# Three of four MLP halves with seven block products instead of eight, and the partial sums copied between PSUM banks

## The chip, the cores and the metric

The kernel runs on all 8 cores of one Trainium2 chip, every core with its own 2048 prompt tokens and 16 sample tokens and the same weights. The metric is the device time of the slowest core, in microseconds. Most executions of a kernel agree within a few tenths of a per cent. In some, the cores of one die, or of both, run at a lower granted TensorE clock and the time is some per cent to 18% longer; such runs are called slow and are left out.

## The reference, cut to what matters

```python
D_MODEL, SEQ, DEPTH = 1024, 2048, 2        # D_FF = 4 * D_MODEL
for l in range(DEPTH):
    h = rmsnorm(x, norm_mix[l])
    mixed = even_layer(h, ...) if l % 2 == 0 else odd_layer(h, ...)   # pool + recurrence / short convolution
    x = x + mixed
    h = rmsnorm(x, norm_mlp[l])
    x = x + jnp.square(jax.nn.relu(h @ ff_w1[l])) @ ff_w2[l]          # the part that changes
return rmsnorm(x, norm_final), ...
```

The first output is the prompt's result after the final norm; the others are the sample group's result and the states.

## The kernel before

The program writes its own instruction order: small Python generators yield operations, each with an estimated duration, and a list scheduler picks which one goes next on its engine. `MMG` is a group of matmuls into one PSUM bank, `ACT` an operation of ScalarE, `TT` a two-tensor operation of VectorE.

```python
# the MLP before: up projection, per 512 hidden columns (s) and 512 tokens (t)
for n in range(4):
    k = (yield Alloc(SB))[0]
    yield MMG([(bank(k), ring[:, sl, kc * 512 + n * 128:kc * 512 + (n + 1) * 128],
                hT[:, kc, tokslice(t)], kc == 0, kc == 7) for kc in range(8)], [B_ring[sl], hTb(t)], [B_ps[k]])
    def ev(...):
        yield ACT(hb[n], bank(k), AF.Relu, [B_ps[k]], [Bh[n]])
        banks.give(k)
        yield TT(hb[n], hb[n], hb[n], ALU.mult, [Bh[n]], [Bh[n]], fast=True)      # the square
# down projection: per block of 128 tokens 2 x 4 matmuls of 128x512, added to x_sb by VectorE
# ...
def main():
    yield from outproj(0, U_WO, 1, "mix", range(8), True)
    mlp(0, U_FF0, 1, 2, (0, 1), (0, 1), hid_a, True)          # layer 0, first 1024 tokens
    # ...
    yield from outproj(1, U_WO, 1, "mix", range(8, 17), False)
    mlp(1, U_FF0, 1, 2, (2, 3, 4), (4, 2, 3), hid_b, False)   # layer 0, second 1024 tokens and the sample tokens
    # ...
    yield from conv()
    yield from outproj(1, U_OO, 3, "cmix", range(17), False)
    mlp(1, U_FF1, 3, 4, (0, 1, 2, 3, 4), (4, 0, 1, 2, 3), hid_b, False)   # layer 1, all tokens
```

## Time and profile before

| | before |
|---|---|
| median of 13 runs | 1563.57 us (fast runs 1560.92 to 1565.59) |
| TensorE busy | 96% of the span, 1495.8 us |
| VectorE, ScalarE busy | 59%, 38% |
| weights read by the GpSimd queue | 74.00 MB, 27.1% of the queue's 16 engines |

The span can be cut into five stages at matmuls that are easy to find: the first and longest (recurrence, first half of layer 0), then the second half of layer 0's MLP ("X"), the convolution and its output projection, layer 1's MLP ("Y") and the tail. The windows of the kernel before, slowest core; the columns are length, then busy time and number of PE, PEld, DVE, ACT and POOL, then clock, DMA share and GB/s:

```profile
0.00:603.20 603.20, 553.34 (x3878) 299.41 (x3878) 426.92 (x781) 334.11 (x716) 159.38 (x176) 0.98 0.51 107
603.20:849.70 246.50, 243.75 (x1689) 121.34 (x1688) 117.99 (x158) 57.34 (x110) 17.99 (x34) 0.99 0.39 69
849.70:1090.80 241.10, 236.66 (x1378) 114.33 (x1376) 139.95 (x236) 91.61 (x169) 9.53 (x18) 1.00 0.21 38
1090.80:1554.20 463.40, 461.96 (x2684) 219.75 (x2680) 234.42 (x297) 102.48 (x202) 13.76 (x26) 1.00 0.21 44
1554.20:1563.60 9.40, 0.11 (x1) 0.00 (x0) 5.16 (x5) 3.11 (x8) 0.00 (x0) 0.68 0.55 224
```

In X and Y, which the change concerns, TensorE is busy for all but 2.8 and 1.4 us. These two stages are 710 of 1564 us.

### The profile page before, as it was taken

What the parts mean: (1) busy time and instruction counts of PE and PEld (TensorE: products, weight loads), DVE (VectorE), ACT (ScalarE), POOL (GpSimd) and SP (SyncE); (2) the same over time, 40 slices, a digit from 0 to 9 for tenths busy, and PEclk for the clock granted to TensorE, in tenths of its full rate; (3) what the DMA queues carried; (4) which work ended last, traced back from release to release, by engine and by line L of the source; (5) the groups of instructions that cost most, each with busy time, mean ns of one, the idle gap of its engine ahead of it and who ended that gap; (6) DMA issues with size and microseconds to landing.
All of it is one profiled execution on the core that took longest, in us unless ns stands there. A gap on an engine that the chain in (4) does not pass through costs nothing.

```text
span 1563.6 us, 24713 instructions; the slowest of 8 cores (1553.1 to 1563.6 us)
## 1 busy us (share of the span) xinstructions
PE 1495.8 (96%) x9620; PEld 754.8 (48%) x9620; DVE 924.4 (59%) x1475; ACT 588.7 (38%) x1201; POOL 200.7 (13%) x254
## 2 busy tenths in 40 slices
PE   3888899999999999999998999999999999999997
PEld 2555455654444445444454444445444444444453
DVE  4799788877545565444446655556444444444457
ACT  4767588864211174111116222256211111111135
POOL 1143533333200000000000000000000000000000
PEclk9899899999999999999999999999999999999999
DMA  6843144388743532443442012330231132031013
GB/s 157 179 85 64 61 89 95 76 200 181 162 86 56 91 70 55 73 84 62 74 69 41 15 27 50 54 69 1 54 54 28 27 54 40 16 55 28 1 56 162
DMA packets 57070, 113.39 MB, mean 73 GB/s; under 512 B 5822, under 2 KB 32556, under 8 KB 56940
## 3 DMA queue, kind: packets, MB, share of 16 engines
q0 software_dynamic: 21344, 74.00, 27.1%
q1 hardware_dynamic: 33996, 37.48, 7.9%
q8 instruction: 79, 1.29, 0.4%
q10 hardware_dynamic: 1616, 0.33, 0.1%
q14 instruction: 35, 0.29, 0.1%
HBM read 170.31 MB, written 15.54 MB: 119 GB/s over the span
## 4 chain that ended last, share of the span: by engine, by line
PE 85%; DVE 7%; DMA 4%; ACT 2%; issue 1%; ACTq 1%; SPq 0%; POOL 0%; DVEq 0%; POOLq 0%
PE pp L523 83%; DMA ring<-wst 2%; PE pp L533 2%; DVE x_sb L492 1%; DVE x_sb L504 1%; DMA mixT<-xs 1%; DVE hT L492 1%; DVE arena L492 1%; ACT arena L479 1%; ACTq L538 1%; ACT x_sb L479 1%; DVE arena L504 1%; DVE x_sb L848 0%; DVE gsm L492 0%; DMA arena<-st_pool 0%
## 5 line engine op out<-in xcount | busy, mean ns | idle before, releaser
L523 PE MATMUL pp<-hT,ring 128*128 128x512 f16 (+1 forms) x4304 | 800.4, 340 | 5.5 <-DMA ring<-wst 3.5
L523 PEld LDWEIGHTS pp<-hT,ring 128*128 128x128 f16 x4304 | 357.9, 98 | 401.5 <-issue 17.8
L492 DVE TENSOR_TENSOR x_sb<-x_sb,pp 128x1024 f32<-128x1024 f32 (+1 forms) x384 | 377.6, 986 | 163.4 <-PE pp L523 159.7
L479 ACT ACTIVATE arena<-pp 128x512 f16<-128x512 f32 (+5 forms) x320 | 181.8, 573 | 619.5 <-PE pp L523 593.4
L523 PE MATMUL pp<-ring,arena 128*128 128x512 f16 x1536 | 340.7, 380 | 3.6 <-DVE arena L492 3.6
L523 PEld LDWEIGHTS pp<-ring,arena 128*128 128x128 f16 x1536 | 150.1, 98 | 185.8 <-issue 6.1
L492 DVE TENSOR_TENSOR arena<-arena 128x512 f16<-128x512 f16 (+1 forms) x206 | 90.8, 441 | 244.0 <-ACT arena L479 243.9
L523 PE MATMUL pp<-ring,mixT 128*128 128x512 f16 x1024 | 231.5, 379 | 3.2 <-DVE x_sb L492 2.6
L538 POOL DMA_DIRECT2D ring<-wst x145 | 78.2, 544 | 1043.3 <-PE pp L523 952.6
L523 PEld LDWEIGHTS pp<-ring,mixT 128*128 128x128 f16 x1024 | 97.6, 98 | 115.3 <-issue 5.4
L480 ACT ACTIVATE arena<-x_sb 128x1024 f16<-128x1024 f32 x64 | 67.5, 1054 | 62.5 <-DVE x_sb L492 46.7
L479 ACT ACTIVATE mixT<-pp 128x512 f16<-128x512 f32 x64 | 38.1, 595 | 131.8 <-PE pp L523 131.7
L492 POOL TENSOR_TENSOR x_sb<-x_sb 128x512 f32<-128x512 f32 (+6 forms) x60 | 73.9, 1231 | 82.2 <-ACT x_sb L479 17.6
L492 DVE TENSOR_TENSOR hT<-pp,gcols_s 128x1024 f16<-128x1024 f16 x64 | 76.9, 1218 | 11.1 <-PE pp L533 11.1
L492 DVE TENSOR_TENSOR mixT<-mixT 128x512 f16<-128x512 f16 x64 | 31.4, 492 | 74.8 <-ACT mixT L479 74.8
L492 DVE TENSOR_TENSOR arena<-pp,arena 128x512 f32<-128x512 f32 (+1 forms) x57 | 39.0, 687 | 42.9 <-PE pp L523 35.6
L479 ACT ACTIVATE x_sb<-x_sb 128x512 f32<-128x512 f32 (+3 forms) x98 | 54.1, 558 | 24.5 <-DVE x_sb L492 15.7
L504 DVE SCALAR_TENSOR_TENSOR arena<-arena,convwf_s 128x512 f32<-128x512 f32 x64 | 47.8, 751 | 20.7 <-ACT arena L479 19.4
L479 ACT ACTIVATE arena<-arena 128x512 f32<-128x512 f32 x88 | 54.3, 622 | 4.9 <-DVE arena L504 3.8
L479 ACT ACTIVATE arena<-x_sb,nrm 128x1024 f16<-128x1024 f32 x48 | 54.4, 1142 | 0.8
L523 PE MATMUL pp<-ring,hT 128*128 128x128 f16 (+1 forms) x832 | 53.4, 223 | 0.5 <-DVE hT L492 0.5
L523 PEld LDWEIGHTS pp<-ring,hT 128*128 128x128 f16 (+1 forms) x832 | 49.3, 99 | 4.0 <-issue 2.1
(134 smaller groups left out, 800.9 us busy)
## 6 DMA issues: line engine op xcount, KB each, us to landing
ring<-wst POOLq DMA_DIRECT2D x137, 512.0 KB, 7.3
x_sb<-xp SPq DMA_DIRECT2D x28, 512.0 KB, 8.6
yp<-x_sb SPq DMA_DIRECT2D x16, 512.0 KB, 2.6
x_sb<-st_hgrn SPq DMA_DIRECT2D x24, 256.0 KB, 3.1
nhs<-x_sb SPq DMA_DIRECT2D x24, 256.0 KB, 2.6
ring<-wst POOLq DMA_DIRECT2D x8, 256.0 KB, 7.2
arena<-gfin SPq DMA_DIRECT2D x1, 512.0 KB, 4.0
nhp<-arena SPq DMA_DIRECT2D x4, 64.0 KB, 1.5
```

What stands on the lines that cost most here:

```text
L479: return e.activation(out=out, in_=in_, func=func, bias=bias, scale=scale)
L480: return e.activation(out=out, in_=in_, func=func, bias=bias, scale=scale, accum_out=accum)
L492: return Op(eng, lambda e: e.tensor_tensor(out=out, in0=in0, in1=in1, op=op), R, W, occ, occ + 0.08)
L504: return Op("dve", lambda e: e.scalar_tensor_tensor(out=out, in0=in0, scalar=scalar, in1=in1, op0=op0, op1=op1), R, W, occ, occ + 0.08)
L523: ins = e.matmul(o, l, r, start=s, stop=t)
L533: ins = e.transpose(out=o, in_=i, identity=idn)
L538: fns = [(lambda e, o=o, i=i: e.dma_start(out=o, in_=i)) for (o, i) in pairs]
```

## The change

The intent is fewer matmuls. A product of two matrices cut into 2 x 2 blocks takes eight block products; Strassen's method in Winograd's form takes seven, and pays with sums of blocks. Here one level of it is used for X and Y. A "quad" of four 128x512 outputs takes 7 x 4 = 28 matmuls instead of 32. Sums of weight blocks and of activation blocks are made on VectorE ahead of the matmuls. The sums behind them are mostly made in PSUM: a product that two outputs share stays in its bank, ScalarE copies it to a second bank, and the next product accumulates onto the copy. One product per quad goes to SBUF and is added by VectorE, with a custom instruction that also clamps.

```diff
+        def quad(prods, evac, pre=None, nxt=None):
+            def bits(k):                      # sets the written bits of a bank that gets a copy
+                if not B_ps[k].full:
+                    yield MMG([(bank(k), identh[:, :], identh[:, :].unsqueeze(1).broadcast_to([128, 4, 128]), True, True)],
+                              [B_const], [B_ps[k]])
+            def copy(k, src):
+                yield from bits(k)
+                yield ACT(bank(k), bank(src), AF.Copy, [B_ps[src]], [B_ps[k]])
+            # ... products 1, 5 | copy | 6 | copy | 2, 7 | next quad's 1 | copy | 3 | 4
+        def wmlp(tag, l, seq, n_in, n_out, smp, gates):
+            # comb1: weight blocks, four sums of 512 a quad      comb2: w2 blocks, four sums of 2048 a group
+            # combh: activations, four sums of 2048 a half       combs: hidden columns, eight sums of 1024 a group
+                        if what in ("12", "22"):
+                            yield Op("dve", lambda e: e._custom_dve(TENSOR_ADD_SAT, out=v, in0=bank(k), in1=gst(n), s0=3e38, s1=0.0), ...)
+        def later_norms(n, blocks, gate_):    # norms of the other half's blocks, made during the last group of a half
+        def warm(on, off):                    # while on, matmuls into a spare bank fill the holes of the planned order
 # ...
-            mlp(0, U_FF0, 1, 2, (0, 1), (0, 1), hid_a, True)
+            mlp(0, U_FF0, 1, (0, 1), hid_a)
-            mlp(1, U_FF0, 1, 2, (2, 3, 4), (4, 2, 3), hid_b, False)
+            wmlp("X", 0, [1], 1, 2, 1, dict(w1c=(), t=(m0,), ...))
+            S.spawn(later_norms(2, range(0, 8), up(("X", "ff2", 2))), FINPRIO)
-            mlp(1, U_FF1, 3, 4, (0, 1, 2, 3, 4), (4, 0, 1, 2, 3), hid_b, False)
+            wmlp("Y", 1, [0, 1], 3, 4, 0, dict(w1c=op3[0:8], t=op3[0:8], ...))
+            S.spawn(later_norms(3, range(8, 16), up(("Y", "ff2", 2))), FINPRIO)
+        S.spawn(warm(up(("op1", 14)), up(("X", "u", 0))), 0)
+        S.spawn(warm(up(("X", "u", 15)), up(("h2", 7), ("X", "done"))), 0)
+        S.spawn(warm(up(("op3", 15)), up(("Y", "u", 0))), 0)
```

Around it, weights come in blocks of 512 KB (layer 1's twice, once per half), banks are no longer reserved in pairs, results are added 512 wide, and the convolution's weights are loaded in another order. This surrounding is called the frame below.

## The prediction

> **What bounds the kernel now.** I first read the busy table of the page and the chain that ended last, then the stages as windows, then single groups of instructions.
>
> ```profile
> PE 1495.8 (96%) x9620; PEld 754.8 (48%) x9620; DVE 924.4 (59%) x1475; ACT 588.7 (38%) x1201; POOL 200.7 (13%) x254
> PEclk9899899999999999999999999999999999999999
> PE 85%; DVE 7%; DMA 4%; ACT 2%; issue 1%; ACTq 1%; SPq 0%; POOL 0%; DVEq 0%; POOLq 0%
> ```
>
> TensorE (PE) is busy 96% of the span at nearly full granted clock, and 85% of the chain is PE. A busy PE need not be at its peak, so I asked for the chain in order of time and for two stages, the second pass of the layer-0 MLP (611 to 833 us) and the layer-1 MLP (1097 to 1544 us).
>
> ```profile
> 611.45 221.77 PE pp L523 x1488
> 840.72 0.68 DVE arena L492 x2
> 841.39 0.14 issue
> 841.53 8.98 PE pp L523 x56
> 1096.94 404.83 PE pp L523 x2344
> ```
>
> ```profile
> 1097.00:1544.00 447.00, 447.00 (x2545) 211.78 (x2545) 221.63 (x283) 92.77 (x179) 12.43 (x24) 1.00 0.20 42
> 611.50:833.00 221.50, 221.50 (x1488) 108.20 (x1487) 103.61 (x140) 42.66 (x80) 14.81 (x28) 1.00 0.39 70
> ```
>
> The window columns are length, then busy time and count of PE, PEld, DVE, ACT, POOL, then clock, DMA share, GB/s. In both MLP stages PE never stops; VectorE (DVE) is half idle, ScalarE (ACT) 80% idle, DMA at 0.2 to 0.4. One matmul is dated from the timeline:
>
> ```profile
> 1210.53 7.07 PE L523 MATMUL pp<-hT,ring 128*128 128x512 f16 x32
> 1212.51 0.60 ACT L479 ACTIVATE arena<-pp 128x512 f16<-128x512 f32 x1 [8.84 <-PE pp L523]
> 1213.14 0.43 DVE L492 TENSOR_TENSOR arena<-arena 128x512 f16<-128x512 f16 x1 [1.80 <-ACT arena L479]
> 1217.43 7.07 PE L523 MATMUL pp<-ring,arena 128*128 128x512 f16 x32
> ```
>
> 32 matmuls start 6.90 us before the next 32, so one costs 0.2158 us. This stage can be shortened only by fewer matmuls, and that is what the change does.
>
> **What the Trainium skill says.** "TensorE: Matmul & The Clock Gate", Part 1, gives 215.7 ns start to start for 512 columns on a warm clock; the 0.2158 us agree. "VectorE: DVE Perf Modes", section on the perf-mode tier table, puts tensor_tensor at 2x for 16-bit operands in SBUF (1224 ns for 2048 elements) and at 1x with a PSUM operand. The trace agrees:
>
> ```profile
> L492 DVE TENSOR_TENSOR x_sb<-x_sb,pp 128x512 f32<-128x512 f32 x168 | 113.8, 684 | 21.0 <-PE pp L523 17.3 <-PE pp L533 1.0
> L492 DVE TENSOR_TENSOR arena<-arena 128x512 f16<-128x512 f16 x192 | 81.5, 425 | 243.9 <-ACT arena L479 243.9
> L479 ACT ACTIVATE arena<-pp 128x512 f16<-128x512 f32 x192 | 114.5, 597 | 515.1 <-PE pp L523 515.0
> ring<-wst POOLq DMA_DIRECT2D x137, 512.0 KB, 7.3
> ```
>
> "PSUM — Partial Sum Buffer", section on the four PSUM rules, says that ACT and DVE writes leave the written bits alone and that a matmul without the start flag adds where the bit is set. The change rests on this (it copies a partial sum to another bank and accumulates onto it). No trace of before shows it; I take the result as correct. "SBUF — State Buffer", section "Who interferes with whom", says tensor_tensor takes only the read half of the port pair that it shares with GpSimd, so the added combinations should not stop the POOL-issued weight loads (inferred there; not shown here).
>
> **The change part by part.** It is Strassen's method in Winograd's form, one level deep: 7 products instead of 8, for the layer-0 MLP on the second 1024 tokens ("X") and the whole layer-1 MLP ("Y"), three of the four MLP halves. The first half of layer 0, which runs beside the recurrence, stays.
>
> Removed: a half has 512 matmuls for each of the two projections. The new unit, a quad, does with 7 x 4 = 28 matmuls what took 32. There are 32 quads in a half, 96 in all, so 96 x 4 = 384 matmuls x 0.2158 = 82.9 us go from PE, all on the path. The small sample-token matmuls keep their number (16 x 16 and 4 x 64 per layer).
>
> Added on ACT: three PSUM-to-PSUM copies in every quad, at an estimated 0.60 us each (the eviction's duration). In the up projection a quad also has one copy of a partial sum and two relus, 6 x 0.60 = 3.6 us of the 28 x 0.2158 = 6.04 us that PE takes, before its share of four squares (0.43 us on DVE, about 0.6 on ACT); with three of four on ACT 5.4 us, 89%. In the down projection it is 1.8 us, 30%.
>
> Added on DVE, per group of 1024 hidden columns (8 quads, 48.3 us of PE): 16 weight combinations of 512 (0.425), 4 of 2048 and 8 of 1024. From the 425 and 684 ns I take a fixed 0.16 us and 0.27 us per 512 at 2x, so about 1.22 and 0.69 us: 6.8 + 4.9 + 5.5. Then 8 custom add-and-clamp reads of PSUM at 0.69 (5.5), 24 residual adds of 0.684 (16.4), four or five squares (1.9), 1.2 for the activation combination. Sum 42.2 of 48.3 us, 87%; the trace shows back-to-back DVE starts 0.06 to 0.08 us closer than the durations, so some 80%. Before it was 50%. Neither engine exceeds PE, but both come close in the up projection.
>
> Added DMA: Y reads its weights twice. A group loads 8 x 512 KB; the POOL queue took 27.1% of 1563.6 us for 74 MB, 5.7 us per MB, so 24 of 48 us. Bandwidth suffices; but four loads issued at once (about 13 us) stand in front of a w1 load that has some 16 us, so it is near.
>
> Latency on the path. A copy's loop is PE to ACT 0.25 us (8 x 0.2158 after 1210.53 is 1212.26; ACT starts at 1212.51), 0.60, and 0.14 back (the issue piece of the chain): 0.99 us. Inside a run of quads two products (1.73 us) cover it: nothing, unless another ACT operation is in front. A run's first quad covers it with one product (0.86): 0.13 to 0.6. Two such starts a group, 24 x 0.3 = 7 us. From up to down projection the last relu, square and four combinations take about 0.25 + 0.6 + 0.43 + 2.8 + 0.14 = 4.2 us, and the next group's first quad (6.0) plus one product covers it: I take 1 us per group for queueing, 12 us.
>
> Ends of stages. X needs all eight norms and four combinations of 2048 (4.9 us) before the second product that runs; before, the stage started after four norms, and the last transposed norm of this outproj came at 612.7, 9.5 us after the last matmul of its outproj: +10 us. X to conv, with eight late norms pushed into the last group: +4. Between Y's halves the combination cannot be done early and nothing covers the hand-over: +5. End of X and of Y without a next quad as cover: +2 each. The tail gets shorter: before, four 1024-wide adds and four final scalings queue on DVE after the last matmuls (1547.2 to 1559.9); after, two blocks per 6 us: -5. Dummy matmuls put into X's start and end and Y's start keep the clock up; they fill idle time only.
>
> Sum: -82.9 + 7 + 12 + 10 + 4 + 5 + 4 - 5 = -45.9, that is 1518 us.
>
> **The rivals.** (1) PE stays the bound throughout, the author's order hides nearly everything: -82.9 + 10 (X's start) + 5 is 1497. For it: 20% slack on DVE, and instruction order fixed from durations close to the trace's. Against: three latency-bound copies per quad behind an 89% busy ACT. (2) ACT and DVE become the bound of the up projection: 3 us more per group as the copies queue, 36 us over my sum, 1554. For it: 89 and 87%. Against: the down projection has slack and the 8 banks allow work ahead. (3) A weight load arrives late in each group, 2 us each: 1542. For it: 13 of 16 us; against: DMA share under half. (4) A granted clock that falls, as stalls let the array idle: 5% of 580 us is 29 us, 1547; against it, stalls of 1 us are short and the page shows 9s in slices with 5 us of idleness.
>
> **Range and chances.** The gain is one number with little doubt, the losses are a sum of small waits between 15 and 85 us. Predicted 1518, range 1490 to 1550. The 2% line is 1533.2; my sum is 15 us below, and the dummy matmuls show waits that somebody measured and tended. Faster by over 2%: 0.73; within 2%: 0.24; slower: 0.03.
>
> **What would show it.** PE at 128x512 with 5632 real matmuls plus dummies instead of 6016; about 201 us for X and 395 to 410 for Y; DVE near 80% and ACT near 70% in both; ACT copies of 0.6 us PSUM to PSUM 288 times; in the waits, PE waiting for ACT's copies (about 7 us) and for the combinations at group changes. It is wrong if the PE idle time inside X and Y exceeds 60 us, if copies take over 0.8 us, if the f16 combinations run at 1x, or if weight loads show as PE's releaser.

## The result and the profile after

The changed kernel is correct and takes 1529.11 us (median of 8 runs, 1524.09 to 1530.06), against 1563.57 of before. The ratio of the two is 0.9774, with a 95% interval of 0.9763 to 0.9784: faster by 2.3%. (A ratio is the mean time of one kernel's fast runs over the mean of the other's fast runs of the same rounds, so it is not quite the ratio of the medians.) The change is 34.5 us, where 45.9 had been predicted; 1529 lies inside the range.

The busy table and the chain that ended last, of the page after:

```profile
PE 1441.5 (95%) x9312; PEld 722.0 (47%) x9334; DVE 1089.1 (72%) x1964; ACT 768.9 (51%) x1558; POOL 223.0 (15%) x286
PE 77%; DVE 7%; DMA 7%; ACT 5%; issue 2%; POOL 1%; SPq 0%; DVEq 0%; ACTq 0%; POOLq 0%
```

TensorE lost 54 us of busy time, not 83, in part because 98 matmuls of 512 columns are not products (below). The same five stages, kernel after, slowest core:

```profile
0.00:601.90 601.90, 548.45 (x3808) 297.56 (x3831) 423.50 (x791) 318.25 (x676) 160.62 (x177) 0.98 0.53 108
601.90:841.30 239.40, 236.67 (x1695) 116.84 (x1693) 180.50 (x320) 136.21 (x271) 16.89 (x31) 1.00 0.39 63
841.30:1073.40 232.10, 232.03 (x1312) 110.79 (x1311) 143.47 (x260) 70.70 (x128) 12.52 (x22) 1.00 0.30 49
1073.40:1511.00 437.60, 423.64 (x2502) 196.72 (x2501) 336.73 (x592) 241.06 (x475) 32.98 (x57) 1.00 0.47 84
1511.00:1522.40 11.40, 0.74 (x4) 0.13 (x2) 4.88 (x7) 2.66 (x8) 0.00 (x0) 0.69 0.44 176
```

X and the convolution stage together lost 16.1 us, Y 25.8; the tail gained 2.0. In Y TensorE now stands still for 14 us; VectorE is busy 77% of it and ScalarE 55%. The groups of instructions that the change added, kernel after, from 560 us on (mean ns of one behind the busy time):

```profile
L493 ACT ACTIVATE pp<-pp 128x512 f32<-128x512 f32 x288 | 166.8, 582 | 209.3 <-PE pp L539 165.2 <-PE pp L541 39.6 <-DVE x_sb L506 2.5
L1697 DVE CUSTOM_DVE_ANT_0 arena<-pp,ring 128x512 f16<-128x512 f32 x84 | 56.2, 686 | 11.6 <-ACT pp L493 7.1 <-PE pp L539 4.3
L506 DVE TENSOR_TENSOR arena<-arena 128x1024 f16<-128x1024 f16 x54 | 37.1, 687 | 2.8 <-ACT arena L493 2.5
L506 DVE TENSOR_TENSOR mixT<-hT,mixT 128x2048 f16<-128x2048 f16 x15 | 18.3, 1220 | 0.0
L1968 PE MATMUL pp<-identh 128*128 128x512 f16 x65 | 16.1, 379 | 0.0
L541 PE MATMUL pp<-identh 128*128 128x512 f16 x33 | 12.5, 384 | 0.0
```

The sizes were as assumed: copies 0.58 us (0.60 assumed), the custom instruction 0.69, the sums 0.69 and 1.22. The last two rows are the matmuls that are no products: 65 that fill holes, and 33 that set the written bits of a bank ahead of a copy. At 0.2158 us start to start the latter are 7.1 us of TensorE, which the prediction had not counted.

TensorE waits, from X to the end, kernel after (engine, line waited for, us in total, times, longest):

```profile
PE pp L539 <- ACT pp L493: 6.8, 12, 1.6
```

So the copies stop TensorE 12 times in 96 quads. The timeline puts nearly all these waits into the groups at the beginnings and ends of a half; between 1339 and 1482 us there is none. A group is 1024 hidden columns; from the start of one down projection to the next it has 224 matmuls, 48.3 us. Three successive such periods of Y, kernel after: the change of halves and the two groups behind it.

```profile
1273.15:1339.24 66.09, 60.36 (x353) 28.52 (x352) 58.52 (x96) 43.54 (x96) 6.51 (x11) 0.97 0.72 145
1339.24:1387.99 48.75, 48.75 (x223) 21.20 (x222) 38.15 (x68) 24.85 (x46) 5.15 (x8) 1.00 0.61 98
1387.99:1436.14 48.15, 48.15 (x223) 21.53 (x222) 38.61 (x69) 25.43 (x46) 3.71 (x7) 1.00 0.40 71
```

The steady groups run at the matmuls' own pace; seven products are worth their full eighth there. The change of halves takes 66 us, with VectorE busy for 58.5 of it: besides the group's own work it makes eight final scalings (10.2 us), four of the late norms' evictions (4.9) and the four sums of activations (4.9). TensorE stands still for 5.7 us, and one of these waits does more than wait:

```profile
1275.73 0.61 PE L551 MATMUL pp<-identh,arena 128*128 128x128 f16 x8 [1.98 <-ACT arena L493]
1276.17 1.75 PE L541 MATMUL pp<-mixT,arena 128*128 128x512 f16 x4
1277.71 1.91 PE L539 MATMUL pp<-mixT,arena 128*128 128x512 f16 x4
```

The eight transposes of a late norm waited 1.98 us for ScalarE's scaling; four matmuls then take 1.75 and 1.91 us instead of 1.02, as the granted clock was halved for 3.4 us from 1276.3 on (the trace's clock record). And the tail on VectorE, kernel after:

```profile
1510.93 2.47 DVE L506 TENSOR_TENSOR x_sb<-x_sb,pp 128x512 f32<-128x512 f32 x4
1515.51 2.48 DVE L518 SCALAR_TENSOR_TENSOR x_sb<-x_sb,nrm,hg 128x1024 f32<-128x1024 f32 x2 [2.10 <-ACT nrm L493]
```

Two blocks finish at the same moment, and their adds, squares and scalings go through one after the other.

### The profile page after: what moved, and what is told of

Same layout as the page of the kernel before. It is cut to its first block, busy times and chain, and to the rows that moved or that the text cites. A ratio compares the mean times of both kernels' runs of the same rounds, so it can differ in the third digit from the quotient of the medians.

```text
span 1522.4 us, 25344 instructions; the slowest of 8 cores (1512.4 to 1522.4 us)
## 1 busy us (share of the span) xinstructions
PE 1441.5 (95%) x9312; PEld 722.0 (47%) x9334; DVE 1089.1 (72%) x1964; ACT 768.9 (51%) x1558; POOL 223.0 (15%) x286
## 4 chain that ended last, share of the span: by engine, by line
PE 77%; DVE 7%; DMA 7%; ACT 5%; issue 2%; POOL 1%; SPq 0%; DVEq 0%; ACTq 0%; POOLq 0%
PE pp L541 51%; PE pp L539 24%; DMA ring<-wst 3%; ACT arena L493 2%; PE pp L551 2%; DVE x_sb L506 2%; ACT arena L494 1%; DMA mixT<-xs 1%; DMA x_sb<-xp 1%; DVE x_sb L518 1%; DVE arena L506 1%; DMA hT<-w2w 1%; ACT x_sb L493 1%; ACT pp L493 1%; DVE mixT L506 1%
## 5 line engine op out<-in xcount | busy, mean ns | idle before, releaser
L541 PE MATMUL pp<-hT,ring 128*128 128x512 f16 (+1 forms) x2704 | 506.6, 336 | 5.7 <-DMA ring<-wst 3.4
L506 DVE TENSOR_TENSOR x_sb<-x_sb,pp 128x512 f32<-128x512 f32 x504 | 335.5, 684 | 127.7 <-PE pp L541 89.9
L541 PEld LDWEIGHTS pp<-hT,ring 128*128 128x128 f16 x2704 | 224.1, 98 | 250.7 <-issue 17.2
L541 PE MATMUL pp<-ring,mixT 128*128 128x512 f16 x1264 | 293.5, 379 | 3.4 <-DVE x_sb L518 1.8
L493 ACT ACTIVATE pp<-pp 128x512 f32<-128x512 f32 x288 | 166.8, 582 | 209.3 <-PE pp L539 165.2
L493 ACT ACTIVATE arena<-pp 128x512 f32<-128x512 f32 (+5 forms) x212 | 117.5, 559 | 159.6 <-PE pp L541 82.1
L539 PE MATMUL pp<-hT,ring 128*128 128x512 f16 x480 | 118.4, 379 | 2.0 <-ACT pp L493 1.0
L493 ACT ACTIVATE arena<-arena 128x512 f32<-128x512 f32 (+1 forms) x176 | 108.8, 625 | 17.6 <-DVE arena L1697 13.0
L506 DVE TENSOR_TENSOR arena<-arena 128x512 f16<-128x512 f16 (+3 forms) x148 | 79.3, 541 | 34.8 <-ACT arena L493 34.3
L539 PE MATMUL pp<-mixT,arena 128*128 128x512 f16 x384 | 95.2, 381 | 0.6 <-ACT pp L493 0.5
L506 DVE TENSOR_TENSOR mixT<-mixT 128x512 f16<-128x512 f16 (+1 forms) x81 | 39.1, 484 | 71.2 <-ACT mixT L493 71.2
L539 PEld LDWEIGHTS pp<-hT,ring 128*128 128x128 f16 x480 | 45.2, 97 | 62.5 <-issue 11.7
```

The lines of the kernel that those rows point to most:

```text
L493: return e.activation(out=out, in_=in_, func=func, bias=bias, scale=scale)
L506: return Op(eng, lambda e: e.tensor_tensor(out=out, in0=in0, in1=in1, op=op), R, W, occ, occ + 0.08)
L539: ins = e.matmul(o, l, r, start=s, stop=t, skip_group_check=True)
L541: ins = e.matmul(o, l, r, start=s, stop=t)
```

## The experiments

Twelve kernels ran, on three chips. "The control" is the changed kernel. Where a kernel has the control's instructions in the control's order, periods between the same two ScalarE instructions can be compared core by core; they are given below for undisturbed cores, worked out from the start times in the traces, and tell more than the whole time, which is a maximum over eight cores.

**The same frame with eight products.** X and Y are computed with plain sums of two products per output; no sums of blocks, no copies, no bit-setting.

```diff
-                    prods = [pr(r.v[:, 0, :], r.B, b11), pr(r.v[:, 1, :], r.B, b21), pr(c.v[:, 2, :], c.rows[2], b22), ...]   # 7
-                    pre = yield from quad(prods, evac, pre, ...)
+                    pairs = [("11", [pr(w11, r.B, b11), pr(w12, r.B, b21)]), ("12", [pr(w11, r.B, t3), pr(w12, r.B, b22)]),
+                             ("21", [pr(w21, r.B, b11), pr(w22, r.B, b21)]), ("22", [pr(w21, r.B, t3), pr(w22, r.B, b22)])]
+                    yield from quad8(pairs, evac)          # likewise in the down projection
```

> The changed kernel's frame (two halves of 1024 tokens with all eight norms first, weights of layer 1 read twice, the first-half norms put late, the tail of two blocks at once) with the plain eight products: no PSUM copies, no combinations, no bit-setting matmuls, 384 matmuls more. Theory A, of my prediction: the method's own waits (first quads of a run, hand-overs between up and down projection) cost some 19 us and its copies and combinations more, so that without them the 82.9 us of matmuls come back by only 50 us or so: about 1575 to 1585. Theory B, from the trace of the changed kernel: groups in the steady part run at PE's floor and the method's own cost is little more than the bit-setting matmuls (7 us) and the combinations at the change of halves (5 us): 1529 + 83 - 12 is about 1600, and the frame alone is worth about +35 us on the kernel before.

Correct, 1560.2 us (1558.98 to 1561.18), ratio to before 0.9975 [0.9961, 0.9989]. Both expectations missed: the frame costs nothing, it gains 4 us. (The scheduler worked the order of this kernel out anew; the custom instruction is gone too, and the fillers are 9 instead of 65.) X, convolution and Y of this kernel, slowest core:

```profile
599.15:846.50 247.35, 247.22 (x1762) 125.44 (x1760) 95.37 (x180) 81.82 (x164) 17.32 (x31) 1.00 0.38 64
846.50:1080.00 233.50, 232.35 (x1312) 110.67 (x1311) 134.89 (x244) 68.67 (x124) 11.97 (x21) 1.00 0.26 45
1080.00:1549.00 469.00, 468.61 (x2732) 224.47 (x2730) 175.88 (x316) 122.42 (x251) 32.85 (x57) 0.99 0.44 80
```

X with the convolution stage is 480.9 us here and 487.6 before: there lies the frame's gain, and no later start of X eats it up. In Y the frame loses: 469.0 us against 463.4. (The first stage, 4.1 us shorter here, says little: it differs by 9 us between the cores of one run of before.) Against this kernel the seven products bring 1560.2 - 1529.1 = 31 us, of the 82.9 us of removed matmuls. By stages 7.9 of 27.6 us arrive in X (247.3 to 239.4) and 31.4 of 55.3 in Y (469.0 to 437.6); the tail and the first stage give 3 back each. So the method's own cost, with the fillers that it needs, is 52 us. The two largest parts that the windows show: the time that fillers take in X (53 of 0.2158 us, 11.4 us) and the time that TensorE stands still in Y (14.0 us, 0.4 here).

**Short bit-setting matmuls.** The 33 matmuls keep their place and planned duration but write 16 of 512 columns. The result is wrong (relative error 1.17).

```diff
-                    yield MMG([(bank(k), identh[:, :], identh[:, :].unsqueeze(1).broadcast_to([128, 4, 128]), True, True)],
-                              [B_const], [B_ps[k]])
+                    op = MMG([(bank(k)[:, 0:16], identh[:, :], identh[:, 0:16], True, True)], [B_const], [B_ps[k]])
+                    op.occ, op.lat, op.full = 512 / 2370.0, 512 / 2370.0 + 0.15, True
+                    yield op
```

> The bit-setting matmuls in front of copies into banks that a partial write had left, shrunk from 512 columns to 16, with the order of all instructions kept (a wrong result on purpose). Theory A: they fill time in which PE waits for the copy anyway: 1527 to 1530. Theory B: PE is the bound where they stand, so their 0.2158 us each is lost on the path: 33 of them, 7 us, about 1522.

1524.07 us (1522.75 to 1525.29), ratio 0.9744 [0.9728, 0.976], about 4.7 us below the control of other rounds (from the two ratios, 0.9744 and 0.9774). Most of the 7.1 us is on the path. The wrong result agrees with the rule that the prediction took from the Trainium skill ("PSUM — Partial Sum Buffer", section on the four PSUM rules): without a matmul over all columns the product overwrites the copy instead of adding to it.

**No fillers.** The 65 dummy matmuls are planned but not emitted.

```diff
             for _ in range(int((start - self.free[eng] - 0.2) / 0.22)):
-                self.streams[eng].append(([], self.filler, False))
+                pass
```

> Without the 65 dummy matmuls that keep PE busy at the stage ends, all else in the same order. Theory A: they stand in idle time only and the granted clock does not fall: 1528 to 1530. Theory B: the idle gap at the start of X (about 6 us) and those at its end bring half clock for some us each: 3 to 8 us slower, 1532 to 1537, with a lower clock in these stretches.

Correct, 1534.84 us (1530.85 to 1536.54), ratio 0.9815 [0.98, 0.9831]: 5.7 us slower. The beginning of X in the control, as a window:

```profile
602.00:622.00 20.00, 19.64 (x175) 10.68 (x173) 16.09 (x24) 8.76 (x18) 2.41 (x5) 1.00 0.49 80
```

The same stretch of this kernel, its slowest core:

```profile
600.00:620.00 20.00, 15.56 (x107) 8.54 (x104) 13.75 (x18) 6.44 (x13) 1.61 (x3) 0.74 0.51 79
```

Without them the granted clock falls to 0.74 of full speed in these 20 us. The fillers do no useful work and are worth their place. On all cores the first period of X goes from 38 to 39 up to 41 to 42 us, that of Y from 34 to 36 to 38, and on five of eight X's last one from 40.2 to 41.5 or more.

**Every copy twice.** The second copy writes the same values once more; planned duration zero.

```diff
                 yield ACT(bank(k), bank(src), AF.Copy, [B_ps[src]], [B_ps[k]])
+                op = ACT(bank(k), bank(src), AF.Copy, [B_ps[src]], [B_ps[k]])
+                op.occ, op.lat = 0.0, -0.06
+                yield op
```

> Every PSUM-to-PSUM copy made twice in a row, order kept nearly the same: 288 ACT instructions of 0.58 us more, 167 us of ACT. Theory A: the copies are near the path (0.99 us loop, 0.86 us of cover in the first quad of a run, ACT near 90% in the up projection): at least 24 x 0.58 + 2 us per group, 35 to 45 us slower. Theory B: two products cover them with 0.7 us to spare, the second copy eats the spare time and only the first quads show it: 10 to 20 us slower.

Correct, 1590.02 us (fast runs 1587.55 to 1590.15), ratio 1.0159 [1.0142, 1.0176]: 61 us slower, more than expected. 288 copies of 0.58 us are 167 us of ScalarE, so more than a third of it reaches the end. TensorE's wait for the copies:

```profile
PE pp L539 <- ACT pp L493: 53.8, 90, 2.2
```

It was 6.8 us in 12 waits. One copy is just hidden; a second one no longer is.

**ScalarE's share of the late norms.** The Square and the scaling of the 16 late norms work on 16 of 1024 columns. Wrong (error 0.97).

```diff
-            yield ACT(junk, xb, AF.Square, [Bx], Bj + Bn, accum=ss)
+            yield same(ACT(junk[:, cs], xb[:, cs], AF.Square, [Bx], Bj + Bn, accum=ss), 1024)    # cs: 16 columns if late
-                yield ACT(junk, xb, AF.Copy, [Bx] + Bn, Bj, scale=rs)
+                yield same(ACT(junk[:, cs], xb[:, cs], AF.Copy, [Bx] + Bn, Bj, scale=rs), 1024)
```

> The changed kernel with the same instructions in the same order; of the norms that are made late (in the last group of X and of the first half of Y, 16 blocks) only the Square and the scaling on ScalarE are cut from 1024 to 16 columns, which takes about 16 x 1.8 us = 29 us of ScalarE from these two places. The result is wrong on purpose. Theory A: the two groups with late norms (56.0 and 56.8 us instead of 52 to 53) and the two stretches behind them are long because ScalarE has the norms in front of the copies that TensorE waits for: the time falls by 8 to 12 us against the changed kernel, to 1517 to 1521 us. Rival B: VectorE is the bound there (58.5 of 66.1 us busy at the change of halves), and the ScalarE work is hidden: the time falls by 2 to 4 us only, to 1525 to 1527 us.

1536.1 us (fast and slow runs 1535.17 to 1757.95), ratio 0.9762 [0.968, 0.9844]: unclear. On this chip most runs, of before too (1578 to 1584), had pairs of cores at clock 0.97: the trace of this kernel shows 0.81 on six cores (three pairs) from 167 to 328 us, before the changed part. It was therefore repeated on another chip.

> The changed kernel with ScalarE's share of the late norms cut to 16 columns again (wrong on purpose). On the last chip its undisturbed cores took 1511.3 us in the mean, 7 us below those of the changed kernel; its whole runs had a pair of cores at a lower clock and settle nothing. Theory A (ScalarE's late norms are on the path): 6 to 10 us below the control. Rival B (VectorE bounds these groups): 2 to 4 us below.

1529.45 us (fast runs 1522.84 to 1530.96), ratio 0.9764 [0.9745, 0.9783], beside a control at 0.9778 [0.9763, 0.9792]: by whole runs not told apart. The periods tell it, and agree on nearly all undisturbed cores of both chips: the one with X's late norms falls from 55.6 to 53.6 us, X's last from 40.2 to 39.7, the one with Y's late norms from 57.1 to 55.0, the change of halves from about 65 to 64.6. That is 5 us: between the two expectations. (The mean core of the fast runs is 1514.5 us, 7.6 below the control's 1522.1 beside it; but that control's trace has stretches at clock 0.81 in Y, told below, which this one's lacks.) A share of the late norms is on the path; the 66 us of the change of halves are not explained by it.

**The sums at the change of halves.** For Y's second half only a quarter of each activation sum is computed. Wrong (error 0.70).

```diff
-                    yield TT(t1.v, b12.v, b11.v, ALU.subtract, b12.B + b11.B, t1.B, fast=True)
+                    cs = slice(0, 4) if i == 0 else slice(0, 1)          # likewise for the other three
+                    yield same(TT(t1.v[:, cs], b12.v[:, cs], b11.v[:, cs], ALU.subtract, b12.B + b11.B, t1.B, fast=True))
```

> The changed kernel with the same order; of the four combinations of 2048 elements of the activations for the second half of Y only a quarter of the columns is computed, which takes 4 x 0.92 = 3.7 us of VectorE out of the change of halves, the one place where nothing else covers them. The result is wrong on purpose. Theory A (VectorE is the bound at the change of halves, and the combination is on the path): the time falls by 3 to 5 us, to 1524 to 1526 us. Rival B (ScalarE's late norms or the copies are the bound): 0 to 1 us.

1540.98 us (1525.75 to 1547.9), ratio 0.9782 [0.9708, 0.9856]: unclear, same chip as above. The period of the change of halves is 62.4 to 65.0 us on eight undisturbed cores (middle 64.2), against 63.8 to 66.2 (middle 65) for the control. So 3.7 us of VectorE gave under 1 us. Neither this sum nor ScalarE's norms alone is the bound there. The traces show why (followed over this period, core by core): of the chain that ended last, the control's part has about 10 us on ScalarE and 11 on VectorE (the rest is mostly TensorE). With ScalarE's norms cut it is 5 and 20, with the sums cut 11 and 4. There are two chains of nearly the same length, and where one is shortened the other takes over.

**The sums of hidden columns twice.** Three of the four sums of 1024 in each part are made twice, each ahead of its original: 72 more of 0.687 us, 4.1 us of VectorE in each of the 12 hand-overs from up to down projection.

```diff
+                        op = TT(s1, a21, a22, ALU.add, Ba21 + Ba22, B1, fast=True)
+                        op.occ, op.lat = 0.0, -HOP
+                        yield op
                         yield TT(s1, a21, a22, ALU.add, Ba21 + Ba22, B1, fast=True)        # likewise s2 and s4
```

> The changed kernel with the same order; three of the four combinations of 1024 elements of the hidden columns are made twice (each first copy just ahead of its second), 72 more of 0.687 us each, 4.1 us more of VectorE in each of the 12 hand-overs from up to down projection; the result stays right. The prediction had put 12 us on these hand-overs, with this chain of combinations on the path. If that were so, each hand-over grows by 2 to 4 us: plus 25 to 50 us, 1554 to 1579 us. Theory A (in the steady groups VectorE has 10 us of slack and the next group's first products cover the hand-over; only the groups at the ends of halves are short of VectorE time): 8 to 9 groups take nothing, three or four take 2 to 4 us: plus 6 to 14 us, 1535 to 1543 us.

Correct, 1579.2 us (fast runs 1575.3 to 1587.47), ratio 1.0044 [0.9954, 1.0135] on the disturbed chip. The mean span of cores at clock 0.98 or more is 1553.8 us, the control's 1518.6 on its chip: about 35 us slower. My theory (6 to 14) fell, and the size is the one expected for a chain on the path (25 to 50). Not all of it is the sums: the trace shows the clock halved for 3.4 us or more three to five times on every core from X on, which costs 1.7 us each time (the control's first trace has one such event on three cores). Every period grows, the steady ones too: 49.7 to 53.6, 46.6 to 49.1 us. Two steady hand-overs of this kernel, core 5:

```profile
1357.94 1.02 PE L539 MATMUL pp<-hT,arena 128*128 128x512 f16 x4 [2.61 <-ACT pp L493]
1399.34 1.02 PE L541 MATMUL pp<-hT,ring 128*128 128x512 f16 x4 [1.91 <-DVE ring L506]
```

The control has no wait at these places. So its steady hand-over is covered, but with only 1 to 2 us to spare (4.1 added, 2 to 4 surfaced): 10 us of free VectorE time in a group are not slack where the chain of sums stands.

**Preferred banks.** A version meant to keep the 4.7 us: a copy's target is chosen among banks whose last matmuls wrote all columns, and 1 of 33 bit-setting matmuls is left. The scheduler works the order out anew.

```diff
-        i = min(range(len(self.avail)), key=lambda j: max(max(b.wt, b.rt) for b in self.avail[j][1]))
+        def key(j):
+            B = self.avail[j][1]
+            t = max(max(b.wt, b.rt) for b in B)
+            return t if full is None else max(t, self.now) + (0.0 if B[0].full == full else 0.5)
```

> A version that may beat both: the changed kernel, but whoever takes a PSUM bank says whether it will be the target of a copy, and then a bank whose last matmuls wrote all of its columns is preferred. One bit-setting matmul is left of 33 (65 fillers as before). The rest of the order is worked out anew by the same program and so differs in details. If the 4.7 us that the run with short bit-setting matmuls gained are to be had in full: 1523 to 1526 us. Rival: by taking another bank than the one that is free the longest, matmuls wait for evictions: 1528 to 1535 us.

Correct, 1537.15 us (1523.79 to 1539.88), ratio 0.9758 [0.9696, 0.982] on the disturbed chip; its cores at clock 0.98 or more average 1514.3 us. It went to the third chip again, with the control beside it.

> The changed kernel itself once more, as the control for the three that run beside it on the same chip, since the last chip gave few runs with all cores at full clock. If its ratio is a property of the kernel and not of the chip: 0.976 to 0.979 of before, 1527 to 1531 us where before has 1564.

> The version with the preferred banks again (one bit-setting matmul instead of 33). On the last chip its undisturbed cores took 1514.3 us in the mean, 4 us below those of the changed kernel. If that holds: 3 to 6 us below the control. If the four microseconds were the chip's: within 1.5 us of the control.

Control: 1528.01 us (1527.3 to 1532.24), ratio 0.9778 [0.9763, 0.9792]. Preferred banks: 1528.44 us (1528.07 to 1531.98), ratio 0.9784 [0.977, 0.9797]. No difference: the removed matmuls did not make the kernel faster. The core means, 1522.1 and 1519.8 us, leave about 2 us. The trace of the new order shows the clock halved at 1252 to 1257 us on five of eight cores and again at 1272 to 1278 us on seven (the control has one such event at 1268 to 1275 us on three cores), so part of the gain may go back into new waits; how much was not separated.

This chip showed something else. The control's Y, core 1:

```profile
1330.00:1345.00 15.00, 15.00 (x59) 6.22 (x58) 12.24 (x24) 8.29 (x17) 1.06 (x2) 0.82 0.88 170
1345.00:1380.00 35.00, 35.00 (x161) 15.49 (x160) 25.27 (x42) 16.16 (x28) 4.07 (x6) 1.00 0.41 62
1380.00:1395.00 15.00, 15.00 (x59) 6.16 (x57) 12.18 (x25) 7.36 (x15) 0.54 (x1) 0.81 0.63 104
1395.00:1423.00 28.00, 28.00 (x130) 12.47 (x129) 21.26 (x33) 11.60 (x21) 1.05 (x2) 1.00 0.21 39
```

Stretches of 15 us at clock 0.81 in the densest part, 59 matmuls where 70 would fit; three of them on cores 0 and 1, two on 2 and 3, shorter ones on the other four. In the two steady periods cores 0 and 1 lost 3 to 4 us each. The kernel before kept a mean clock of 0.990 on this chip (all cores of its fast runs), the control 0.986. The control's ratio is the same as on the first chip all the same.

**Scalings on GpSimd.** The preferred banks, and 12 of the 16 late norms' scalings moved from ScalarE to GpSimd.

```diff
+            elif late and b % 8 < 6:
+                op = TS(junk, xb, rs, ALU.mult, [Bx] + Bn, Bj)
+                yield Op("pool", op.fn, op.R, [op.W, B_gps], 0.15 + 1024 / 465.0, 0.23 + 1024 / 465.0)
```

> A version that may beat all: the preferred banks, and of the 16 late norms' scalings (1.1 us each on ScalarE) 12 go to GpSimd, which is 85% idle, at about twice the time each; the last two of each half stay on ScalarE. The result stays right. If ScalarE is what the late norms cost, half of the 7 us that the cut gained less the longer latency: 1 to 3 us below the version with preferred banks alone. Rival (the longer latency delays the transposes that stand in TensorE's queue): 0 to 4 us above it.

1546.09 us (fast runs 1532.4 to 1553.37), ratio 0.985 [0.9805, 0.9895], and wrong: relative error 0.042 in the first output. The other outputs agree as in the control. Why is open; the version is no candidate. It is slower in any case. One scaling takes 3.2 us where 2.3 were planned, and TensorE waits for it 5 times, 3.4 us in all; but the profiled run also had two cores at clock 0.81 for 156 us in Y, so how much of the 18 us the scalings cost is not shown:

```profile
L518 POOL TENSOR_SCALAR arena<-x_sb,nrm 128x1024 f16<-128x1024 f32 x12 | 38.6, 3215 | 83.1 <-ACT nrm L500 50.6 <-DVE x_sb L513 29.6 <-DVE mixT L513 2.8
```

No version was found that beats the changed kernel beyond the noise.

## Why the prediction was right

The direction, the verdict (faster by over 2%) and the mechanism held; the gain came out 11 us smaller than the predicted number. First, where these 11 us are. The two profiled runs differ by 1563.6 - 1522.4 = 41.2 us; the changed kernel's profiled run was its fastest, 5.0 us under its median, and that of before 1.6 over its own. So 4.7 us of the miss are in the stages and the rest in which run was profiled. The mean core went from 1557.7 (the runs of before beside the first four experiments) to 1518.6 us, 39.1 us; the slowest of eight gained less, as the changed kernel's cores scatter more (standard deviation 5.5 against 3.3 us).

| stage | predicted change, from its terms | measured in the two traces |
|---|---|---|
| X and convolution | -27.6 + 10 + 4 + 2 + 4 x 1.6 = -5.2 | -16.1 |
| Y | -55.3 + 5 + 2 + 8 x 1.6 = -35.5 | -25.8 |
| tail | -5 | +2.0 |

(1.6 us is the 7 + 12 us for copies and hand-overs, spread over 12 groups. The first stage adds -1.3.) X with the convolution came out 10.9 us better than its terms, Y and the tail 9.7 and 7.0 worse. That the sum came so near is in part luck: errors of opposite sign.

- **Removed matmuls, -82.9.** Right, and in steady groups visible as such: 48.15 and 48.75 us for 224 matmuls.
- **Copies 7 us, hand-overs 12 us.** The first number is right as a sum (6.8 us of waiting), but not the place: none in the steady groups of Y's second half, nearly all at the beginnings and ends. The hand-over's 1 us was not there: 48.75 and 48.15 us leave at most 0.5. The doubled sums show how near it was, with 1 to 2 us to spare.
- **X's start 10 and end 4 + 2.** Over-all better than that for a reason that the prediction did not see: the frame with eight products shows X and convolution 6.8 us shorter than before, as waits went away (TensorE stood still for 7.2 us in the two stages before, for 1.3 in that kernel). The start itself was sized too high: from the output projection's sample matmuls to the unbroken run of products it takes 10.7 us (601.89 to 612.60, 4 product matmuls among them), before 8.1 (603.17 to 611.28, 16 among them), so some 5 us by this estimate. All this hides a mis-sized end: X's last period took 39.4 us where an estimate from its 32.2 us of work leaves 7, and the late norms put 2.0 + 0.5 us on it through ScalarE.
- **Change of halves 5.** The largest mis-sized term. From the period before it (56.8 us instead of some 52.5) and the change itself it is about 14 us, by this estimate: 236 matmuls are 50.9 us, the small matmuls and transposes about 5, which leaves 10 of the 66.1 (5.7 of them standing still, 1.7 the halved clock, 1.1 five bit-setting matmuls), and 4 come from the late norms' period. The prediction counted the uncovered sums and forgot that the same stretch holds eight final scalings and the late norms. VectorE's and ScalarE's work there form two chains of nearly the same length: cutting either alone brought under 1 us there, and the traces show the other one taking over. What cutting both would bring was not run.
- **Ends of X and Y, 2 each.** Y's last period took 28.9 us for 111 matmuls of 24.0: 4.9.
- **Tail, -5.** Failed in sign: +2.0. The prediction took the queue of adds and scalings before (1547.2 to 1559.9) as if it all came behind the last matmul; only 5.6 us of it did. After, two blocks end at once and take 6.3 us from the last matmul (1511.7) to the end of the last scaling (1518.0).
- **Not counted:** 33 bit-setting matmuls, 7.1 us of TensorE and 4.7 on the path by experiment. The fillers were counted as free, which is right; without them the time grows by 5.7 us.
- **The rivals.** ScalarE and VectorE as the bound of the up projection (1554) did not happen, but both doublings, +61 and +35 us, show it one operation away. A late weight load did not show: no transfer releases TensorE from X on. (Two small slips in the working: four loads are 12 us, not 13, by its own 24 for eight, and rival 1 sums to 1496, not 1497.) A falling clock (1547) did not happen on the first chip, and in part on the third.
- **The list of what would show it.** Right: 5632 matmuls of 128x512 besides the dummies, 288 copies at 0.58 us, the f16 sums at twice the speed (1.22 us for 2048), VectorE busy 75% in X and 77% in Y, 6.8 us of waiting for copies, 16.7 us of idle TensorE in X and Y (60 would have spoken against it). Wrong: ScalarE near 70% (57% and 55%), and Y, which became 25.8 us shorter where 447 to 395 or 410 was said.

## What to carry to other kernels

When a method removes matmuls and pays with work beside them, steady state tells little: it ran at TensorE's pace with VectorE at 80%, and the loss sat where stages meet, where norms, final scalings and sums fall together. Count everything that each engine does in those stretches, not only what the change adds. Average slack is not slack on a chain: 10 us of free VectorE time per group hid only 1 to 2 us more in the hand-over. And let a planned order be judged by periods between the same instructions, core by core, when whole runs scatter by as much as the effect. And ask, after a cut that brings nothing, which chain has taken over.

## What the Trainium skill lacked or had wrong

- "TensorE: Matmul & The Clock Gate", Part 1, on the peak-current limiter: it says that a die goes to 13/16 of the clock when three of its cores run dense matmuls, and stays there while the load lasts, and advises to budget for that. Here, in the traced runs, all eight cores ran dense matmuls at a granted clock of 1.00 for most of the time. 0.81 appeared on one chip in stretches of 15 us on pairs of cores (4 to 9 us on others; in one kernel 156 us on one pair), and on another chip in one stretch of 161 us, on three pairs of one run and on one pair of another. The value agrees, and in these runs it did not last as long as the load. In slow runs a whole die had a mean clock of 0.825 (1757.95 us) or 0.837 (1811.58 us); none of them was traced, so there it may have lasted.
- The same page gives the return to half clock after an idle window of about 3.4 us. Here a wait of 1.98 us, with no longer one near it, was followed by 3.4 us at half clock (1276.3 us, core 2); the other two such events from X to the end of Y were on cores 0 and 5 of that run. The length agrees. The 3.4 us before the event hold some 0.8 us of matmuls, the wait and eight transposes; how much of a window may be busy that still counts as idle, Part 1 does not say, and no run here separates it.
- "ScalarE: Activation LUTs", section "Step-by-step: what each stage is for", says that PSUM is the faster destination, without a time. A copy of 128x512 from PSUM to PSUM took 582 ns, a relu of the same size from PSUM to SBUF 597 ns in the kernel before (another function, and f16 out instead of f32).
- No page has the duration of a custom VectorE instruction that reads PSUM: 686 ns for 512 elements, like a tensor_tensor with a PSUM operand (684).
- "PSUM — Partial Sum Buffer", section on the four PSUM rules, was right on the written bits (error 1.17 when they were set for 16 of 512 columns only). It doesn't price the remedy: 0.2158 us of TensorE for each bank, 33 times here.
